# Row normalisation on one Trainium2 core: tiles of 16 rows in three buffers, with sums and scaling shared by two engines

## The chip, the core and the metric

The kernel runs on one NeuronCore of one Trainium2 chip. The metric is the device time of the slowest (here the only) core in microseconds (us), as the median of several executions. VectorE is called DVE in the profile, ScalarE is ACT, and the sequencers that issue transfers are SPq (loads) and ACTq (stores). The page counts 16 DMA engines for the core; on the load and the store queue they moved 67.11 MB each between HBM and the on-chip memory SBUF.

## The reference

```python
x = np.random.randn(32, 512, 1024).astype(np.float32)
sums = np.sum(np.abs(x), axis=-1, keepdims=True)
return (x / (sums + 1e-8)).astype(np.float32)
```

There are 16384 rows of 1024 numbers, so 67.11 MB are read and 67.11 MB are written. Each of the 128 partitions gets 128 rows. Below, "one row" of a tile is one row in each partition: 128 x 4 KiB = 0.524 MB.

## The kernel before

A tile takes 12 rows per partition (the last tile 8), in a ring of 4 buffers. DVE sums the absolute values of all rows and scales two thirds of them. ACT scales the rest and issues the stores.

```python
R = 12
BUFS = 4
...
def piece(flat, i):                      # a tile is one contiguous stretch of HBM:
    a, k = P * sum(rows[:i]), rows[i]    # partition p has k consecutive rows of it
    return flat[a : a + P * k, :].rearrange("(p r) d -> p r d", p=P)
...
# normalize(x_tile, 0, k, k - k // 3):
nc.vector.tensor_reduce(out=s[:, :k], in_=x_tile[:, r0 : r0 + k, :], ..., apply_absolute_value=True)
nc.vector.tensor_scalar_add(out=s[:, :k], in0=s[:, :k], scalar1=EPS)
nc.vector.reciprocal(out=inv[:, :k], in_=s[:, :k])
nc.vector.tensor_mul(...)                # rows r0 .. r0 + kv on DVE
for r in range(kv, k):
    nc.scalar.activation(out=row, in_=row, func=Copy, scale=inv[:, r : r + 1])
...
for i, k in enumerate(rows):
    x_tile = sbuf.tile([P, R, d], FP32)
    nc.sync.dma_start(out=x_tile[:, :k, :], in_=piece(x_flat, i))
    normalize(x_tile, 0, k, k - k // 3)
    nc.scalar.dma_start(out=piece(out_flat, i), in_=x_tile[:, :k, :])
```

Of the kernel before, what the change touches and what calls it, by code (L numbers as in the profile page):

```python
# [1 line left out]

# [4 lines left out]

FP32 = mybir.dt.float32
EPS = 1e-8


@with_exitstack
def kernel(
    ctx: ExitStack,
    tc: tile.TileContext,
    x: bass.AP,
    out: bass.AP,
):
    nc = tc.nc
    P = nc.NUM_PARTITIONS  # L20

    x_flat = x.flatten_outer_dims()
    out_flat = out.flatten_outer_dims()
    n, d = x_flat.shape


    R = 12
    BUFS = 4
    per_partition = n // P
    assert n % P == 0  # L30
    rows = [R] * (per_partition // R)
    if per_partition % R:
        rows.append(per_partition % R)

    def piece(flat, i):
        a, k = P * sum(rows[:i]), rows[i]
        return flat[a : a + P * k, :].rearrange("(p r) d -> p r d", p=P)

    sbuf = ctx.enter_context(tc.tile_pool(name="sbuf", bufs=BUFS))
    stats = ctx.enter_context(tc.tile_pool(name="stats", bufs=4))  # L40

    def normalize(x_tile, r0, k, kv):

        s = stats.tile([P, R], FP32)
        nc.vector.tensor_reduce(  # L45
            out=s[:, :k],
            in_=x_tile[:, r0 : r0 + k, :],
            axis=mybir.AxisListType.X,
            op=mybir.AluOpType.add,
            apply_absolute_value=True,  # L50
        )
        nc.vector.tensor_scalar_add(out=s[:, :k], in0=s[:, :k], scalar1=EPS)  # L52
        inv = stats.tile([P, R], FP32)
        nc.vector.reciprocal(out=inv[:, :k], in_=s[:, :k])  # L54
        nc.vector.tensor_mul(  # L55
            out=x_tile[:, r0 : r0 + kv, :],
            in0=x_tile[:, r0 : r0 + kv, :],
            in1=inv[:, :kv].unsqueeze(2).to_broadcast([P, kv, d]),
        )
        for r in range(kv, k):  # L60
            row = x_tile[:, r0 + r, :]
            nc.scalar.activation(  # L62
                out=row,
                in_=row,
                func=mybir.ActivationFunctionType.Copy,
                scale=inv[:, r : r + 1],
            )

    with tc.manual_schedule():
        for i, k in enumerate(rows):  # L70
            x_tile = sbuf.tile([P, R, d], FP32)
            nc.sync.dma_start(out=x_tile[:, :k, :], in_=piece(x_flat, i))  # L72
            normalize(x_tile, 0, k, k - k // 3)
            nc.scalar.dma_start(out=piece(out_flat, i), in_=x_tile[:, :k, :])  # L74


# [1 line left out]
_INS = ['x']  # L78
_OUTS = [((32, 512, 1024), 'float32')]


# [23 lines left out]
```

## Time and profile before

| | before |
|---|---|
| time, median of 3 (range) | 317.11 us (317.05 to 318.38) |
| span of the profiled run | 315.7 us |
| DVE, ACT busy | 235.8 us, 46.1 us |
| bytes, mean rate | 134.23 MB, 425 GB/s |

The span is what the profiler saw of one execution. An engine's busy time is the sum of its instructions. Here every compute engine has a busy share below 100% (DVE 75%, ACT 15%), and the DMA share is 0.97 to 1.01 from 2 to 312 us, so the kernel waits for bytes. The prediction shows the lines.

### The profile page before, as it was taken

How to read it: one execution, taken by the hardware profiler on the slowest of the kernel's cores; microseconds unless marked ns; L12 is line 12 of the kernel's file. 1: busy time of each engine (PE TensorE's matmuls, PEld its weight loads, DVE VectorE, ACT ScalarE, POOL GpSimd, SP SyncE). 2: the span in 40 equal slices, each digit the busy share in tenths (PEclk: the TensorE clock that was granted, in tenths of full speed). 3: DMA queues.
4: the chain of work that ended last, by engine and by line, in shares of the span. 5: the costliest groups of instructions: out<-in, count | busy, mean ns of one | idle time of the engine just before them, and what ended most of it. 6: DMA issues, size and time to landing. Idle time of an engine off the chain costs nothing.

```text
span 315.7 us, 205 instructions
## 1 busy us (share of the span) xinstructions
DVE 235.8 (75%) x44; ACT 46.1 (15%) x43; POOL 0.2 (0%) x4
## 2 busy tenths in 40 slices
DVE  0069999999999699739947991997399469979400
ACT  0010501303105003200500050032005000502000
POOL 0000000000000000000000000000000000000000
DMA  8999999999999999999999999999999999999996
GB/s 318 467 405 436 455 380 423 405 473 423 399 479 417 405 479 411 423 461 411 455 436 405 473 417 405 473 423 399 486 406 411 479 413 421 438 455 411 455 401 274
DMA packets 3169, 134.23 MB, mean 425 GB/s; under 512 B 352, under 2 KB 352, under 8 KB 352
## 3 DMA queue, kind: packets, MB, share of 16 engines
q1 hardware_dynamic: 1584, 67.11, 49.7%
q10 hardware_dynamic: 1584, 67.11, 49.1%
q14 instruction: 1, 0.01, 0.0%
HBM read 67.11 MB, written 67.11 MB: 425 GB/s over the span
## 4 chain that ended last, share of the span: by engine, by line
another core or an unknown queue 36%; DMA 31%; DVE 26%; SPq 0%; issue 0%; DVEq 0%; ACTq 0%
DMA x_tile<-in_x_dram 15%; DMA out_dram<-x_tile 15%; DVE s L45 15%; DVE x_tile L55 10%; SPq L72 0%; DVE inv L54 0%; DVE s L52 0%; DVEq L54 0%; ACTq L74 0%
## 5 line engine op out<-in xcount | busy, mean ns | idle before, releaser
L45 DVE TENSOR_REDUCE s<-x_tile 128x12 f32<-128x12288 f32 (+1 forms) x11 | 138.2, 12562 | 58.0 <-DMA x_tile<-in_x_dram 58.0
L55 DVE TENSOR_TENSOR x_tile<-x_tile,inv 128x8192 f32<-128x8192 f32 (+1 forms) x11 | 93.5, 8498 | 0.4
L62 ACT ACTIVATE x_tile<-x_tile,inv 128x1024 f32<-128x1024 f32 x42 | 44.9, 1137 | 226.3 <-DVE inv L54 226.3
L62 ACT ACT_TABLE_LOAD x1 | 1.3, 1283 | 18.7 <-DMA x_tile<-in_x_dram 18.7
L54 DVE RECIPROCAL inv<-s 128x12 f32<-128x12 f32 (+1 forms) x11 | 2.5, 225 | 0.9
L52 DVE TENSOR_SCALAR s<-s 128x12 f32<-128x12 f32 (+1 forms) x11 | 1.9, 173 | 0.4
L89 POOL MEMSET const-bfloat16-1.0<- 128x1 bf16 x1 | 0.1, 101 | 0.0
L89 POOL MEMSET const-uint8-127<- 128x1 uint8 x1 | 0.1, 101 | 0.0
L89 POOL MEMSET const-float32-0.0<- 128x1 f32 x1 | 0.1, 98 | 0.2 <-issue 0.2
L89 POOL MEMSET const-float32-1.0<- 128x1 f32 x1 | 0.1, 98 | 0.0
## 6 DMA issues: line engine op xcount, KB each, us to landing
x_tile<-in_x_dram SPq DMA_DIRECT2D x10, 6144.0 KB, 34.9
out_dram<-x_tile ACTq DMA_DIRECT2D x10, 6144.0 KB, 51.3
x_tile<-in_x_dram SPq DMA_DIRECT2D x1, 4096.0 KB, 30.4
out_dram<-x_tile ACTq DMA_DIRECT2D x1, 4096.0 KB, 19.1
```

The costliest lines, as they stand in the source:

```text
L45: nc.vector.tensor_reduce(out=s[:, :k], in_=x_tile[:, r0 : r0 + k, :], axis=mybir.AxisListType.X, op=mybir.AluOpType.add, apply_absolute_v ...
L52: nc.vector.tensor_scalar_add(out=s[:, :k], in0=s[:, :k], scalar1=EPS)
L54: nc.vector.reciprocal(out=inv[:, :k], in_=s[:, :k])
L55: nc.vector.tensor_mul(out=x_tile[:, r0 : r0 + kv, :], in0=x_tile[:, r0 : r0 + kv, :], in1=inv[:, :kv].unsqueeze(2).to_broadcast([P, kv, d]),)
L62: nc.scalar.activation(out=row, in_=row, func=mybir.ActivationFunctionType.Copy, scale=inv[:, r : r + 1],)
L89: nc = _bacc.Bacc("TRN2", target_bir_lowering=False, num_devices=1)
```

## The change

The intent is to take work off DVE. The absolute sums are shared: DVE sums three fifths of the rows and ACT the rest, with an Abs activation per row that accumulates its output. Scaling is halved between the two. Tiles grow to 16 rows in three buffers (the same 48 rows in flight), with a first and a last tile of 8 rows, so that stores start early and the last compute is short.

```diff
-    R = 12
-    BUFS = 4
+    R = 16
+    BUFS = 3
-    rows = [R] * (per_partition // R)
-    if per_partition % R:
-        rows.append(per_partition % R)
+    rows = [R // 2] + [R] * (per_partition // R - 1) + [R // 2]
...
+        kv = k * 3 // 5
+        km = k // 2
         nc.vector.tensor_reduce(
-            out=s[:, :k],
-            in_=x_tile[:, r0 : r0 + k, :],
+            out=s[:, :kv],
+            in_=x_tile[:, :kv, :],
...
+        for r in range(kv, k):
+            nc.scalar.activation(
+                out=junk[:, :],                 # in PSUM, never read
+                in_=x_tile[:, r, :],
+                func=mybir.ActivationFunctionType.Abs,
+                accum_out=s[:, r : r + 1],
+            )
...
         nc.vector.tensor_mul(
-            out=x_tile[:, r0 : r0 + kv, :],
+            out=x_tile[:, :km, :],
...
-        for r in range(kv, k):
+        for r in range(km, k):
```

More of the change, by code (lines that the diff above doesn't have):

```diff
@@ L24 @@
     n, d = x_flat.shape
-    R = 12
-    BUFS = 4
+    R = 16
+    BUFS = 3
     per_partition = n // P
-    assert n % P == 0
-    rows = [R] * (per_partition // R)
-    if per_partition % R:
-        rows.append(per_partition % R)
+    assert n % P == 0 and per_partition % R == 0
+    rows = [R // 2] + [R] * (per_partition // R - 1) + [R // 2]
     def piece(flat, i):
@@ L40, with normalize @@
     stats = ctx.enter_context(tc.tile_pool(name="stats", bufs=4))
-    def normalize(x_tile, r0, k, kv):
+    psum = ctx.enter_context(
+        tc.tile_pool(name="psum", bufs=1, space=bass.MemoryType.PSUM)
+    )
+    junk = psum.tile([P, d], FP32)
+    def normalize(x_tile, k):
+        kv = k * 3 // 5
+        km = k // 2
         s = stats.tile([P, R], FP32)
         nc.vector.tensor_reduce(
-            out=s[:, :k],
-            in_=x_tile[:, r0 : r0 + k, :],
+            out=s[:, :kv],
+            in_=x_tile[:, :kv, :],
             axis=mybir.AxisListType.X,
@@ L51, in normalize @@
         )
+        for r in range(kv, k):
[4 more added lines that the diff above has]
+                accum_out=s[:, r : r + 1],
+            )
         nc.vector.tensor_scalar_add(out=s[:, :k], in0=s[:, :k], scalar1=EPS)
@@ L55, in normalize @@
         nc.vector.tensor_mul(
-            out=x_tile[:, r0 : r0 + kv, :],
-            in0=x_tile[:, r0 : r0 + kv, :],
-            in1=inv[:, :kv].unsqueeze(2).to_broadcast([P, kv, d]),
-        )
-        for r in range(kv, k):
-            row = x_tile[:, r0 + r, :]
+            out=x_tile[:, :km, :],
+            in0=x_tile[:, :km, :],
+            in1=inv[:, :km].unsqueeze(2).to_broadcast([P, km, d]),
+        )
+        for r in range(km, k):
+            row = x_tile[:, r, :]
             nc.scalar.activation(
@@ L72 @@
             nc.sync.dma_start(out=x_tile[:, :k, :], in_=piece(x_flat, i))
-            normalize(x_tile, 0, k, k - k // 3)
+            normalize(x_tile, k)
             nc.scalar.dma_start(out=piece(out_flat, i), in_=x_tile[:, :k, :])
```

## The prediction

> **What bounds the kernel now.** I began with the busy shares and the DMA line of the page, and asked which of the two could fill 315.7 us.
>
> ```profile
> DVE 235.8 (75%) x44; ACT 46.1 (15%) x43; POOL 0.2 (0%) x4
> DMA packets 3169, 134.23 MB, mean 425 GB/s; under 512 B 352, under 2 KB 352, under 8 KB 352
> ```
>
> No compute engine is full. The kernel moves 134.23 MB, 67.11 in and 67.11 out, at a mean of 425 GB/s. Whether that mean has holes in it is told by the windows view, where the last two columns are the busy share of the 16 DMA engines and their GB/s (the first are the stretch, its length, then busy us of DVE, ACT, POOL):
>
> ```profile
> 0.00:2.00 2.00, 0.00 (x0) 0.00 (x0) 0.20 (x4) 1.00 1.05 295
> 2.00:40.00 38.00, 21.27 (x4) 5.55 (x5) 0.00 (x0) 1.00 0.97 418
> 40.00:60.00 20.00, 19.90 (x5) 4.27 (x4) 0.00 (x0) 1.00 1.01 413
> 60.00:120.00 60.00, 56.66 (x10) 8.53 (x8) 0.00 (x0) 1.00 1.01 437
> 120.00:180.00 60.00, 46.09 (x9) 8.53 (x8) 0.00 (x0) 1.00 1.00 434
> 180.00:240.00 60.00, 45.69 (x12) 8.70 (x9) 0.00 (x0) 1.00 1.00 433
> 240.00:280.00 40.00, 30.92 (x6) 8.37 (x8) 0.00 (x0) 1.00 1.00 433
> 280.00:312.00 32.00, 15.27 (x4) 2.19 (x2) 0.00 (x0) 1.00 0.99 429
> 312.00:316.00 4.00, 0.00 (x0) 0.00 (x0) 0.00 (x0) 1.00 0.15 66
> ```
>
> From 60 us to 280 us the transfers never stop: share 1.00, about 434 GB/s. All bytes at 434 GB/s are 134.23 / 0.434 = 309.3 us, so only 315.7 - 309.3 = 6.4 us of the span are not bytes at the steady rate. They sit at the two ends: the start and the loads-only stretch (2 to 60 us, slightly under rate), and the last 4 us at 66 GB/s. The second check is the tile period, read from the timeline of DVE:
>
> ```profile
> 139.07 12.95 DVE L45 TENSOR_REDUCE s<-x_tile 128x12 f32<-128x12288 f32 x1 [6.76 <-DMA x_tile<-in_x_dram]
> 168.08 12.95 DVE L45 TENSOR_REDUCE s<-x_tile 128x12 f32<-128x12288 f32 x1 [6.80 <-DMA x_tile<-in_x_dram]
> 197.08 12.95 DVE L45 TENSOR_REDUCE s<-x_tile 128x12 f32<-128x12288 f32 x1 [6.78 <-DMA x_tile<-in_x_dram]
> ```
>
> Starts are 29.0 us apart. A tile of 12 rows (one row here is 128 x 4 KB = 0.524 MB) in and out is 24 x 0.524 = 12.58 MB, which at 434 GB/s is 29.0 us: the period is the bytes alone. DVE works 22.1 us of it and waits 6.8 us for a load. The tail could still be a compute path, so I read the timeline there:
>
> ```profile
> 277.61 0.34 ACTq L74 DMA_DIRECT2D out_dram<-x_tile  x1
> 279.65 8.69 DVE L45 TENSOR_REDUCE s<-x_tile 128x8 f32<-128x8192 f32 x1 [2.13 <-DMA x_tile<-in_x_dram]
> ...
> 288.88 6.56 DVE L55 TENSOR_TENSOR x_tile<-x_tile,inv 128x6144 f32<-128x6144 f32 x1
> 295.53 0.34 ACTq L74 DMA_DIRECT2D out_dram<-x_tile  x1
> ```
>
> The last load lands at 279.6, and the last store is issued at 295.5, after 15.9 us of reduce, small steps and scaling. But the store issued at 277.6 (12 rows, 14.5 us alone) stands behind a remainder of the one before, and the windows show share 0.99 from 280 to 312. So the last tile's compute hides behind stores, though the chain of waits passes through it.
>
> [...] when a load and a store are both queued I give each half the rate. The trace agrees roughly: loads of 6.29 MB land in a median of 34.9 us, about twice the 14.5 us of one alone plus latency. [...] The pitch goes from 48 KiB (12 rows) to 64 KiB here; the trace before cannot show the new pitch. [...] the trace has 1137. I take as much for the new Abs activations, with some 0.1 us on top for the accumulator, an allowance of mine.
>
> **The change part by part.** The durations come from the groups by form:
>
> ```profile
> L45 DVE TENSOR_REDUCE s<-x_tile 128x12 f32<-128x12288 f32 x10 | 129.5, 12950 | 55.9 <-DMA x_tile<-in_x_dram 55.9
> L55 DVE TENSOR_TENSOR x_tile<-x_tile,inv 128x8192 f32<-128x8192 f32 x10 | 86.9, 8692 | 0.3
> L62 ACT ACTIVATE x_tile<-x_tile,inv 128x1024 f32<-128x1024 f32 x42 | 44.9, 1137 | 226.3 <-DVE inv L54 226.3
> L45 DVE TENSOR_REDUCE s<-x_tile 128x8 f32<-128x8192 f32 x1 | 8.7, 8685 | 2.1 <-DMA x_tile<-in_x_dram 2.1
> ```
>
> *Sums.* A reduce costs (12950 - 8685) / 4 = 1066 ns a row plus 158 ns. Of 16 rows DVE takes 9: 9.75 us. ACT takes 7 at about 1.2 us: 8.4 us, beside it. *Scaling.* DVE takes 8 rows, 8.69 us as in the row above; ACT 8 rows at 1.07 us back to back, 8.5 us, beside it. Between the phases lie 0.5 us (31.58 to 32.08 in the timeline of before). A 16-row tile thus takes 9.75 + 0.5 + 8.7 = 19.0 us, where 12 rows took 22.1. An 8-row tile takes 4 rows each: about 4.8 + 0.5 + 4.4 = 9.7 us; the first one 1.3 us more for the table load.
> *Busy time.* DVE: 7 x (9.75 + 8.69) + 2 x (4.42 + 4.42) + 9 x 0.4 = 150 us instead of 236. ACT: 57 sums at 1.2 plus 64 scalings at 1.07 plus 1.3 = 138 us instead of 46. All of it lies beside transfers.
> *Transfers.* The bytes don't change. There are 18 issues instead of 22. Period of a tile: 32 x 0.524 / 0.434 = 38.7 us, of which 19.0 are compute.
> *Buffers.* 3 x 16 rows hold as many rows as 4 x 12. Load i+3 waits for store i. I followed the queues by hand at 1.208 us a row, half rate each when both have work, 1.9 us from last byte to start of work (16.7 computed for the first load of before, 18.6 seen). First load landed 13.8; first store issued about 25 instead of 40.9; third load still running when the first store has landed (47), so no hole at the start. In the steady state, from the end t of store i-1: load i+2 is issued at t+2, load i+1 finishes its remaining 3 rows at t+7.3 and is seen at t+9.2, its compute ends at t+28.2, and store i, already queued, ends at t+38.7. So the next store is queued 10 us early, and the DMA engines always have a store or a load. At the end: last load seen at about 277, last store issued at about 287, the 16-row store ahead of it ends at about 301. Again queued, by 14 us.
> *Sum.* First bytes at about 2.2 us + 256 + 256 rows: 134.23 MB / 0.434 = 309.3 us, to 311.5; the final receipt and end as before (312.5 to 315.7), 3 us; start imbalance of 0.5 to 1.5 us. Span 315.2, times about 1.4 us more outside the span (317.11 - 315.7): 316.6 us. The 86 us of DVE time that go buy next to nothing.
>
> **Rivals.** (1) *The earlier first store and the shorter last compute are gains.* They are 15 us and 6 us sooner; were both on the path, 317 - 21 = 296 us. Against it: 309.3 us of bytes at a share of 1.00. What can be won is only part of the 6.4 us at the ends. (2) *Three buffers starve the queues.* Then each of six or seven tiles would show a hole; 2 us each makes 330 us. For it: a load now waits for a store of 16 rows, and one buffer fewer is in flight. Against: 10 us of margin. Even if the ACT sums ran after the DVE sums (they share the tile s), compute would be 27.4 us and the margin still about 2 us; rows of x_tile are already scaled by both engines at once in the trace, so parts of a tile are tracked. (3) *The 64 KiB rows move at another rate.* Each per cent is 3 us; nothing in the trace speaks for it. (4) *ACT becomes a bound and delays its own store issues*, as they stand in its stream behind 16 activations: 16.9 us of ACT work in 38.7 us, no.
>
> **Range and chances.** A DMA-bound kernel whose bytes stay is fixed to within its ends: 309.3 + 4.4 at best is 313.7 of time, and the repeats of before reach 318.4. I take 315.0 to 318.8. Faster by over 2% means below 310.8, some 1.5 us over the bytes alone: 1%. Slower by over 2% (323.5) needs rival 2 or 3: 3%.
>
> **What would show it.** Right: share about 1.00 and 433 to 437 GB/s from 60 to 280 us; reduces 38.7 us apart; DVE near 150 and ACT near 138 us busy; DVE waits for loads some 20 us a tile; last store issued over 5 us before the one ahead of it lands. Wrong: stretches with a share below 0.95 between 60 and 280 us, placed after a store's landing (rival 2), or a share of 1.00 at fewer GB/s (rival 3); sums one after the other on DVE and ACT would show a smaller margin only.

## The result, and the profile after

| | before | after |
|---|---|---|
| time, median of 4 (range) | 317.18 us (317.05 to 318.38) | 321.60 us (319.84 to 321.73) |
| span of the profiled run | 315.7 us | 319.9 us |
| DVE, ACT busy | 235.8, 46.1 us | 150.6, 134.3 us |
| mean rate over the span | 425 GB/s | 420 GB/s |

The ratio is 1.0118 with a 95% interval of 1.0075 to 1.0161. Ratios here are the mean time of one kernel's fast runs over that of the other's of the same rounds, so not quite the ratio of the quoted medians. The change is "same" at the 2% mark, but it is 4.4 us slower, where 0.6 us faster was predicted, and it lies outside the predicted range.

The first lines of the page of the changed kernel, busy shares and DMA packets:

```profile
DVE 150.6 (47%) x36; ACT 134.3 (42%) x179; POOL 0.2 (0%) x4
DMA packets 2594, 134.24 MB, mean 420 GB/s; under 512 B 288, under 2 KB 288, under 8 KB 288
```

The compute side came out as intended. The groups of instructions by form (line, engine, operation, shapes, count, then busy us and mean ns, then idle time before them) say so in detail:

```profile
L50 DVE TENSOR_REDUCE s<-x_tile 128x9 f32<-128x9216 f32 x7 | 68.3, 9755 | 124.7 <-DMA x_tile<-in_x_dram 124.7
L74 ACT ACTIVATE x_tile<-x_tile,inv 128x1024 f32<-128x1024 f32 x64 | 67.5, 1135 | 15.9 <-DVE inv L66 15.9
L58 ACT ACTIVATE junk<-x_tile 128x1024 f32<-128x1024 f32 x57 | 58.6, 1027 | 151.1 <-DMA x_tile<-in_x_dram 149.6
L58 ACT ACTIVATION_READ_ACCUMULATOR junk<-x_tile 128x1 f32 x57 | 10.6, 186 | 0.0
```

The reader sees 9.755 us for nine rows (9.75 predicted), and 57 sums on ACT that cost two instructions each. Both engines wait over 120 us in all for loads, so neither is a bound.

The windows view of the changed kernel has the DMA share and GB/s in its last two columns:

```profile
60.00:120.00 60.00, 35.18 (x8) 30.63 (x42) 0.00 (x0) 1.00 1.01 436
120.00:180.00 60.00, 21.44 (x5) 18.77 (x25) 0.00 (x0) 1.00 1.01 435
180.00:240.00 60.00, 36.67 (x8) 32.12 (x44) 0.00 (x0) 1.00 0.97 422
240.00:280.00 40.00, 19.31 (x5) 16.90 (x23) 0.00 (x0) 1.00 1.01 433
280.00:312.00 32.00, 9.86 (x5) 9.24 (x13) 0.00 (x0) 1.00 1.00 430
312.00:320.00 8.00, 0.00 (x0) 0.00 (x0) 0.00 (x0) 1.00 0.12 53
```

By this view the engines are busy as before. (A window's edge cuts packets of 1 MB over the 16 engines, so 0.97 and 422 in one window prove no hole.) What is new is the last line: after 312 us little moves, for seven more microseconds. In the kernel before, the span ended at 315.7.

The timeline of DVE shows the tile period and the end:

```profile
103.52 9.75 DVE L50 TENSOR_REDUCE s<-x_tile 128x9 f32<-128x9216 f32 x1 [20.06 <-DMA x_tile<-in_x_dram]
...
261.59 9.75 DVE L50 TENSOR_REDUCE s<-x_tile 128x9 f32<-128x9216 f32 x1 [20.52 <-DMA x_tile<-in_x_dram]
```

```profile
280.73 0.34 ACTq L86 DMA_DIRECT2D out_dram<-x_tile  x1
292.49 1.03 ACT L58 ACTIVATE junk<-x_tile 128x1024 f32<-128x1024 f32 x1 [12.12 <-DMA x_tile<-in_x_dram]
292.49 4.42 DVE L50 TENSOR_REDUCE s<-x_tile 128x4 f32<-128x4096 f32 x1 [11.85 <-DMA x_tile<-in_x_dram]
...
302.17 0.34 ACTq L86 DMA_DIRECT2D out_dram<-x_tile  x1
```

Four periods take 158.1 us, 39.5 us each where 38.7 was predicted, and the last load is seen at 292.5 where about 277 was predicted. Yet no view shows an idle DMA engine.

**Where the 4 us are.** The compute starts on a tile when all 16 DMA engines have done their share of its load (the last load's 16th increment of the semaphore came at 292.47 us, and DVE started at 292.49), and the trace keeps the moment of each engine's increment. None of the views prints them; I read them from the records of the trace. Stores of the changed kernel, with the median engine and the delay of the last one, in us:

```
store of tile        1      2      3      4      5      6      7      8 (last)
median engine     97.96 136.61 175.26 213.90 250.11 281.53 303.28 313.19
last - median      0.70   1.95   2.75   3.23   6.61   7.23   6.09   5.85
```

In the kernel before, the last store lands at 313.56 in the median and 1.11 us later on its last engine (stores in mid-run: 0.4 to 0.5 us; loads 2.4 to 2.8 us, which does not grow). So the median engine of the changed kernel is even 0.4 us earlier than before, with a period of 38.65 us as predicted, and the whole loss is in a few engines that fall behind: 319.04 against 314.67 us for the last landing, 4.4 us.

An engine falls behind by slow packets. Each packet here is one partition's contiguous run (the seven 16-row tiles of 128 partitions, in and out, are 1792 packets of 64 KiB in the trace). In the changed kernel a packet of 64 KiB takes 2.418 us in the median, 27.1 GB/s. After 62 us, 69 packets took longer, by up to 0.93 us, with 14.6 us of excess in sum over the 16 engines. In the kernel before (packets of 48 KiB, 1.815 us) there are 12 such packets with 1.0 us. In what follows this sum is called the **slow time**: the excess of all packets that start after 62 us over the median of their length, where it is over 15 ns. (Before 62 us the excess is 29.6 us in the kernel before and 23.8 in the changed one, so the loss does not come from there.) Sorted into chains by their ends and starts (packets of one engine follow each other within 10 ns), the packets show 16 engines with 72 load and 72 store packets each, with work from the first byte to the last, nearly without a gap, and the latest one with 7.0 us of excess, 1.4 of it before 62 us.

### The profile page after: what moved, and what is told of

Read it like the earlier page. It is cut to its first block, busy times and chain, and to the rows that moved or that the text cites. A ratio compares the mean times of both kernels' runs of the same rounds, so it can differ in the third digit from the quotient of the medians.

```text
span 319.9 us, 321 instructions
## 1 busy us (share of the span) xinstructions
DVE 150.6 (47%) x36; ACT 134.3 (42%) x179; POOL 0.2 (0%) x4
## 2 busy tenths in 40 slices
DMA packets 2594, 134.24 MB, mean 420 GB/s; under 512 B 288, under 2 KB 288, under 8 KB 288
## 4 chain that ended last, share of the span: by engine, by line
another core or an unknown queue 49%; DMA 36%; DVE 7%; ACT 1%; SPq 1%; issue 1%; DVEq 0%; ACTq 0%
DMA x_tile<-in_x_dram 22%; DMA out_dram<-x_tile 13%; DVE x_tile L67 4%; DVE s L50 3%; ACT junk L58 1%; SPq L84 1%; DVE inv L66 0%; DVE s L64 0%; DVEq L64 0%; ACTq L86 0%
## 5 line engine op out<-in xcount | busy, mean ns | idle before, releaser
L50 DVE TENSOR_REDUCE s<-x_tile 128x9 f32<-128x9216 f32 (+1 forms) x9 | 77.1, 8569 | 149.6 <-DMA x_tile<-in_x_dram 149.6
L58 ACT ACTIVATE junk<-x_tile 128x1024 f32<-128x1024 f32 x57 | 58.6, 1027 | 151.1 <-DMA x_tile<-in_x_dram 149.6
L74 ACT ACTIVATE x_tile<-x_tile,inv 128x1024 f32<-128x1024 f32 x64 | 67.5, 1135 | 15.9 <-DVE inv L66 15.9
L67 DVE TENSOR_TENSOR x_tile<-x_tile,inv 128x8192 f32<-128x8192 f32 (+1 forms) x9 | 69.7, 7743 | 0.3
L58 ACT ACTIVATION_READ_ACCUMULATOR junk<-x_tile 128x1 f32 x57 | 10.6, 186 | 0.0
L66 DVE RECIPROCAL inv<-s 128x16 f32<-128x16 f32 (+1 forms) x9 | 2.2, 242 | 0.3
L64 DVE TENSOR_SCALAR s<-s 128x16 f32<-128x16 f32 (+1 forms) x9 | 1.6, 174 | 1.4 <-ACT junk L58 0.6
```

Of the source, the lines that this page charges most:

```text
L50: nc.vector.tensor_reduce(out=s[:, :kv], in_=x_tile[:, :kv, :], axis=mybir.AxisListType.X, op=mybir.AluOpType.add, apply_absolute_value=True,)
L58: nc.scalar.activation(out=junk[:, :], in_=x_tile[:, r, :], func=mybir.ActivationFunctionType.Abs, accum_out=s[:, r : r + 1],)
L67: nc.vector.tensor_mul(out=x_tile[:, :km, :], in0=x_tile[:, :km, :], in1=inv[:, :km].unsqueeze(2).to_broadcast([P, km, d]),)
L74: nc.scalar.activation(out=row, in_=row, func=mybir.ActivationFunctionType.Copy, scale=inv[:, r : r + 1],)
```

## The experiments

Eighteen kernels ran, all correct in their output, each timed beside the kernel before on its chip; the median of before stayed between 317.25 and 317.51 us. "Spread" is the delay of the last engine behind the median in the last store. "Hole" is the time from 4 us to the last store's landing on its median engine in which fewer than 8 of the 16 engines had a packet. The expectations name theories by letters: T and S, the tiles as such; C, the shared compute; P and P2, the length of the packets (64 KiB alone, or long ones in general); B and B2, three large buffers, or only lengths near 64 KiB; F, the instruction fetch; L, engines that read and write in step.

| run | tiles, buffers | packets | time, us | ratio, 95% interval | spread | slow time | hole |
|---|---|---|---|---|---|---|---|
| before | 12 rows, 4 | 48 KiB | 317.11 | | 1.11 | 1.0 | 0.0 |
| after | 16 rows, 3 | 64 KiB | 321.60 | 1.012, 1.008 to 1.016 | 5.85 | 14.6 | 0.1 |
| after_again | 16, 3 | 64 | 321.65 | 1.012, 1.010 to 1.014 | 5.21 | 12.8 | 0.4 |
| e2_old_tiles | 12, 4 | 48 | 317.63 | 1.001, 1.000 to 1.002 | 1.19 | 1.2 | 0.0 |
| g4_tiles_alone | 16, 3 | 64 | 326.91 | 1.029, 1.027 to 1.031 | 0.10 | 58.9 | 7.2 |
| e7_rows12_3 | 12, 3 | 48 | 317.71 | 0.999, 0.996 to 1.003 | 0.08 | 1.3 | 1.4 |
| e6_rows8 | 8, 6 | 32 | 317.23 | 0.999, 0.998 to 1.001 | 1.91 | 1.6 | 0.0 |
| e4_halves | 16, 3 | 32 | 318.88 | 1.005, 1.004 to 1.006 | 1.38 | 24.0 | 0.0 |
| e5_halves_pitch | 16, 3 | 32 | 318.79 | 1.004, 1.003 to 1.005 | 1.57 | 19.3 | 0.0 |
| h3_quarters | 16, 3 | 16 | 318.77 | 1.004, 1.003 to 1.006 | 0.91 | 0.9 | 0.0 |
| m1_pad | 16, 3 | 32 | 318.64 | 1.004, 1.003 to 1.005 | 1.30 | 21.0 | 0.0 |
| m2_nopad | 16, 3 | 64 | 321.09 | 1.012, 1.008 to 1.016 | 3.44 | 28.2 | 1.1 |
| h1_rows14 | 14, 3 | 56 | 319.90 | 1.008, 1.007 to 1.010 | 1.62 | 8.0 | 2.3 |
| g2_early_fetch | 16, 3 | 64 | 321.62 | 1.012, 1.010 to 1.014 | 3.62 | 14.2 | 0.0 |
| e3_rows15 | 15, 3 | 60 | 326.02 | 1.025, 1.021 to 1.029 | 0.10 | 5.0 | 7.3 |
| h2_rows15_tail | 15, 3 | 60 | 334.54 | 1.042, 1.036 to 1.047 | 0.10 | 27.4 | 11.2 |
| h4_rows12_first8 | 12, 3 | 48 | 326.55 | 1.030, 1.028 to 1.031 | 0.09 | 26.6 | 8.6 |
| e9_first12 | 16, 3 | 64 | 325.83 | 1.025, 1.020 to 1.029 | 0.07 | 37.9 | 3.9 |
| k8 | 16, 3 | 64 | 335.03 | 1.055, 1.051 to 1.060 | 3.50 | 142.3 | 0.3 |
| k16 | 16, 3 | 64 | 337.69 | 1.063, 1.058 to 1.067 | 2.07 | 143.6 | 0.0 |

Times are medians of all runs; ratios are of fast runs alone. A run over 1.5% above the fastest of its kernel counts as slow. Three rows hold such runs: e3_rows15 has one (fast median 325.09 us), g2_early_fetch one (321.59), and h2_rows15_tail four of six (its two fast runs took 328.61 and 332.55); of the runs of before beside h1 to h4 one was slow, at 322.02. The slow time of k8 and k16 includes 42 and 86 us of the extra store's own packets.

(In the runs with a hole of 3.9 us or more the spread is 0.07 to 0.10 us: late engines catch up in the hole, as I read it.)

### The changed kernel again

No edit.

> The changed kernel once more, beside the experiments on the same chip. It was 1.2% slower than the kernel before (321.6 against 317.2 us). In its trace the 16 DMA engines finish their part of the last store at 313.2 us in the median and one of them 5.9 us later, where in the kernel before the spread is 1.1 us. If the late engine belongs to the kernel: 319.8 to 321.8 us again, spread of the last store's landings 4 to 7 us. If it was an accident of one chip: about 317 us and a spread near 1 us.

Measured: 321.65 us, a spread of 5.21 us. The late engine belongs to the kernel and is no accident of one run.

### The new compute on the old tiles

```diff
-    R = 16
-    BUFS = 3
+    R = 12
+    BUFS = 4
```

> The new division of sums and scaling over both engines, with the tiles of before (12 rows, 4 buffers). Theory T (the transfers of the 16-row tiles make some DMA engines slow): 317 us as before or up to 0.5 us less, last store's landings within 1.5 us. Theory C (both engines reading and writing the tile slow the transfers): 320 us or more with the late engine there.

Measured: 317.63 us, spread 1.19, slow time 1.2 us. Theory C falls: sharing sums and scaling costs the transfers nothing, and it gains nothing either. The loss comes with the tiles.

### The new tiles with the old compute

The tiles, buffers and order of the change, with DVE summing all rows and scaling two thirds.

> The other half of the change: the tiles of after (8, seven of 16, 8; three buffers) with the compute of before (vector engine sums all rows and scales two thirds). It takes about 29.6 us a tile, just about the margin of a 38.7 us period, so at most small holes. Theory F (an 8 KB instruction fetch, which the trace shows on one DMA engine at 71 us in the changed kernel and at 230 us in the kernel before, puts that engine out of step; with 16-row tiles it then keeps losing time): no fetch near 71 us as ScalarE has few instructions, so no late engine before the fetch (near 200 us or later), spread of the last store's landings under 3 us, 316.5 to 319 us. Theory S (the tiles as such): slow packets from 65 us on as in the changed kernel, 320 us or more.

Measured: 326.91 us. The expectation of theory F was wrong in the time: the only instruction fetch in mid-run came at 294.7 us, as it said, and no store landed over 2.4 us late on its last engine, but the slow time is still 58.9 us, 3.7 us per engine. Besides, there is a hole near the end, in a windows view of this run:

```profile
240.00:288.00 48.00, 38.61 (x8) 10.61 (x10) 0.00 (x0) 1.00 0.99 423
288.00:295.00 7.00, 7.00 (x2) 0.00 (x0) 0.00 (x0) 1.00 0.30 128
```

DVE is busy through the hole: the last 16-row tile takes from 263.9 to 293.6 us, and its store can't be issued before. So the 16-row tiles need the shared compute: with the old compute they cost 9.4 us, with the shared one 4.4. (The shared compute doesn't need the tiles, as the run before showed.)

### Fewer buffers alone

```diff
-    R = 16
+    R = 12
-    rows = [R // 2] + [R] * (per_partition // R - 1) + [R // 2]
+    rows = [R] * (per_partition // R) + [per_partition % R]
```

These are the tiles of before (ten of 12 rows, one of 8) in three buffers.

> The tiles of before (12 rows) and the new compute, but three buffers instead of four. Theory L: the number of buffers matters only through the phase; with mixed reads and writes 317 to 318 us, with engines in step 319 us or more and slow packets in the trace. Theory S in the form that three buffers do it: 320 us or more whatever the phase. A hole in the transfers would need the compute of a tile (14.4 us for 12 rows by the measured row times) to exceed the margin of a period of 29 us; not expected.

Measured: 317.71 us, slow time 1.3 us, a hole of 1.4 us before the last store. Three buffers alone do not make slow packets.

### The length of a row block: 60 KiB

```diff
-    R = 16
+    R = 15
-    rows = [R // 2] + [R] * (per_partition // R - 1) + [R // 2]
+    rows = [11] + [R] * 7 + [12]
```

> Three buffers of 15 rows (a first tile of 11 rows and a last of 12), the rest as in the changed kernel: runs of 60 KiB per partition instead of 64 KiB. Theory P (the 64 KiB run, a power of two, is what slows single packets): 316.5 to 318 us, landings of the last store within 1.5 us. Theory B (three large buffers, transfers of 8 MB in step, whatever their exact length): 320 to 322 us as in the changed kernel.

Measured: 326.02 us, slower than either forecast, so theory P (that exactly 64 KiB is bad) gets no support. But most of the loss is of my making:

```profile
299.00:306.00 7.00, 5.88 (x1) 5.67 (x6) 0.00 (x0) 1.00 0.31 130
```

For 7 us the transfers stand nearly still: the last load was seen at 290.1 us, 7.0 us after its median engine, and a last tile of 12 rows needs 15 us of compute, while the store ahead of it ended at about 299 in the median. I then ran it with another tail:

```diff
+    rows = [8] + [R] * 7 + [7, 8]
```

> The 15-row run again with a tail that leaves no hole: tiles of 8, seven times 15, 7 and 8 rows. The earlier one had 326.0 us, of which a hole of about 7 us in the stores before its last tile of 12 rows was part. Theory P2: 319 to 322 us with slow packets in the trace; theory B2 with 64 KiB alone: 317 to 318.5 us.

Measured: 334.54 us (328.61 and 332.55 in the two fast runs), with a larger hole, so this test of the length failed too:

```profile
304.00:315.00 11.00, 9.22 (x4) 8.86 (x12) 0.00 (x0) 1.00 0.07 31
```

The store of 7 rows was too short to cover the last load and compute. Both runs do show a late engine with 60 KiB packets (7.0 and 6.5 us late in the last load), but their times measure the tail.

### 14 rows

```diff
+    R = 14
+    rows = [8] + [R] * 8 + [8]
```

> Three buffers, tiles of 8, eight times 14, and 8 rows: packets of 56 KiB. Theory P2 (long packets lose, growing with the length): between the 12-row and 16-row times, 318 to 320.5 us. Theory B2 (only the lengths near or at 64 KiB lose): 317 to 318 us. If it is as slow as 16 rows (321 or more), the length between 48 and 56 KiB would be the threshold.

Measured: 319.90 us, between 12 and 16 rows as theory P2 has it. Slow time is 8.0 us; one engine was 7.0 us late in the last load, and a hole of 2.3 us in the stores followed from that.

### A first tile of 8 rows with 12-row tiles

```diff
+    R = 12
+    rows = [8] + [R] * 9 + [4, 8]
```

> Three buffers of 12 rows with a first tile of 8 (tiles 8, nine times 12, 4, 8): packets of 48 KiB, but the short first tile and the pause between the first and second store of the changed kernel. Theory P2: 317 to 318.5 us, no late engine. If the first tile sets off the slow packets: 320 us or more.

Measured: 326.55 us. Until 260 us the slow time is 3.0 us in sum, and no engine falls behind as in the changed kernel, so the early store and the pause after it are not the cause. The time is lost at the end: slow packets of 24 us in sum after 260 us, where 12-, 4- and 8-row transfers meet, and a hole of 8.6 us with the same cause as in the 15-row run (a store of 4 rows covers nothing). As a test of the total time it failed.

### Halves, with and without the pitch

Each load and each store of a 16-row tile becomes two of 8 rows; in the first version each half is contiguous in HBM, in the second a half takes 8 of the 16 rows of every partition.

```diff
-            nc.sync.dma_start(out=x_tile[:, :k, :], in_=piece(x_flat, i))
+            for h, part in halves(x_flat, i):
+                nc.sync.dma_start(out=x_tile[:, h : h + H, :], in_=part)
```

> The 16-row tiles and three buffers stay, but each load and store is two transfers of 8 rows, each with its own contiguous stretch of memory: runs of 32 KiB. Theory P (64 KiB exactly): back to 316.5 to 318 us. If any power of two does it: 319 us or more. Theory B (three buffers of 16 rows): 320 to 322 us, since the buffers and the waits are unchanged.

> As the run with halves, but the layout of the 16-row tile in HBM stays: each transfer takes 8 of the 16 rows of each partition, so packets of 32 KiB at a pitch of 64 KiB. If the packet length (32 KiB) decides: like the halves, about 318.9 us. If the pitch in HBM decides: 320 us or more, like the changed kernel.

Measured: 318.88 and 318.79 us. The pitch in HBM (32 or 64 KiB per partition) makes no difference here: 0.09 us between the medians. The late engine is gone (spreads of 1.4 and 1.6 us). A slow time of 19 to 24 us remains, but it is shared: nearly all of it falls in one episode between 105 and 120 us, in which all engines lose about 1.3 us, and none is late afterwards.

### Quarters

As the halves, with H = R // 4.

> The 16-row tiles and three buffers, each load and store as four transfers of 4 rows: packets of 16 KiB. Halves (32 KiB packets) had 318.9 us. Theory P2: 317 to 318.5 us. If the 16-row tile with its three buffers itself costs the rest, as with the halves: 318.7 us or more.

Measured: 318.77 us with a slow time of 0.9 us. Slow packets are gone, so theory P2 held there; its forecast of the time missed, because packets of 16 KiB cost more per byte in this trace. One takes 0.611 us, and 512 of them per engine at that time less the 4 ns by which neighbours overlap are 310.8 us. For 256 packets of 32 KiB at 1.213 us it is 309.5 us.

### Smaller tiles

```diff
+    R = 8
+    BUFS = 6
+    rows = [R] * (per_partition // R)
```

> The new compute with 16 tiles of 8 rows and 6 buffers: as many rows in flight, packets of 32 KiB. Theory F with the loss growing with the packet length: 317 to 318.5 us and a spread of landings under 2.5 us. If every division into blocks of a power of two rows loses: 319 us or more, as with the halves (318.9).

Measured: 317.23 us, slow time 1.6 us. 8-row tiles match the kernel before.

### Do the engines run in step?

In the changed kernel the 16 engines alternate between load and store together: from 100 to 140 us there are at most one or at least 14 engines in a load packet for 85% of the time. In the kernel before this is 13%. I took this for the cause (theory L) and tried to break it with an extra store.

```diff
+            if i == 1:
+                nc.scalar.dma_start(out=spare[:, :, :], in_=x_tile[:K, :, :])   # K = 8 or 16
```

The spare tensor lies in HBM and is never read.

> The changed kernel with one extra store of 16 rows of 8 partitions to a spare tensor in HBM, issued just before the store of the second tile. It goes to 8 of the 16 DMA engines, one packet of 64 KiB each (2.42 us of their time), and leaves those 8 writing while the other 8 read. Theory L (packets turn slow where all engines alternate between load and store in step; where half read and half write they don't): hardly any slow packets after 65 us (under 2 us in sum over the engines, against 13 and 14 us in the two traces of the changed kernel), and the 8 engines end 2.4 us after the others, at about 315.3 us, so about 318.3 us. Theory S (the slow packets come of the 16-row tiles or the three buffers as such): as many slow packets, 321.6 us or more, up to 324.

> The control: the same extra store, but 16 partitions, so one extra packet on each of the 16 engines; they stay in step. Theories L and S both: slow packets stay (8 us or more after 65 us), a late engine stays, and the time is that of the changed kernel plus 2.4 us, about 324 us. If instead this one too comes to about 319 us, the extra store acts in another way than by the phase, and theory L falls.

Measured: 335.03 and 337.69 us. Both expectations were wrong, and the experiment doesn't decide anything, because the extra store was no simple kick: its packets took 7.4 to 8.1 us (8 partitions) and 7.2 to 8.9 us (16) instead of 2.42. That is 3.0 to 3.7 times as long. I had not expected it, and it is not shown why: stores from so few partitions occur in these two runs alone. The extra store moved what was meant: the pages count 0.52 and 1.04 MB more than that of the changed kernel (134.76 and 135.28 MB), and 8 and 16 more packets under 512 B (296 and 304 against 288, which is 16 for each of its 18 transfers), as for 8 and 16 engines. After this jolt slow packets went on for some 70 us in both, and in the first they came back at 190 us.

As the whole cause, theory L falls by other runs. With 8-row tiles the engines are in step for 65% of the time from 100 to 140 us, with three buffers of 12 rows for 45%, and both have almost no slow packets. And this run has mixed reads and writes from 60 us on, with 37.9 us of slow time:

```diff
+    rows = [12] + [R] * 7 + [4]
```

> The changed kernel with a first tile of 12 rows and a last of 4 instead of 8 and 8. Theory L with the phase set early by the spread of the engines' first packets: if the 48 KiB first packets spread the engines as widely as in the kernel before, reads and writes mix and the time is 316.5 to 318.5 us. If the engines stay in step: 320 to 322 us. Theory S: 320 to 322 us. The share of time in which nearly all engines read, or nearly all write, in the trace tells which.

Measured: 325.83 us. The engines did leave the common step, and it was worse, not better: 34.5 us of the slow time fall between 62 and 100 us. After that, however, slow packets nearly stop. From 100 to 250 us they sum to 0.5 us here (engines in step for 9% of that time), against 5.4 and 6.4 us in the two traces of the changed kernel (63% and 60%). The first 15-row run has 0.5 us too (8%), but the second has 3.1 (12%), and the tiles with the old compute 15.9 (29%). So it is not excluded that long packets keep turning slow while the engines run in step; no run sets the step alone. Some 3.9 us of it are a hole before the last store, as the tail is again small (4 rows).

### The instruction fetch

In both traces of the changed kernel an 8 KiB transfer of the instruction queue comes at 71.0 us and takes 0.309 us on one DMA engine. In the first trace, by the chains of packets, it is that engine which then falls behind. In the second it is not: there the latest engine is one without a fetch, 2.6 us behind at 158 us, when the engine with the fetch was 0.4 behind. In the kernel before the fetch comes at 230.1 us.

```diff
+        for _ in range(55):
+            nc.scalar.activation(out=junk[:, :1], in_=dot[:, :], func=mybir.ActivationFunctionType.Abs)
```

> The changed kernel with 55 one-element activations on ScalarE at the start, where it waits for the first load. They move the first instruction fetch from 71 us into the loads-only stretch before 15 us, and the second from 287 to about 195 us. Theory F: hardly any slow packets between 30 us and 190 us (under 0.5 us in sum; 7 us in the changed kernel), the late engine begins at about 195 us, and the time drops by 1 to 3 us to 318.5 to 320.5. Theory S: slow packets from 65 us on, time unchanged at 321.6.

Measured: 321.62 us with a wide range, 319.96 to 325.60 (the last in the slow state, the fast ones up to 321.73); the profiled run was the fastest of them. The fetches moved to 16.9 and 197.1 us. Slow time between 62 and 180 us was 4.0 us, between those of the two traces of the changed kernel (4.6 and 3.2; the 7 us of the expectation were a wrong sum), though spread over many engines, and an episode of 8.2 us followed at 220 to 230 us. Taking the early fetch away did not give the time back, and the run with the tiles alone had slow packets without any fetch. As the cause of the loss theory F falls.

### The length of the packets alone

The last pair has equal tiles, buffers, transfers, waits and instructions. They differ in one number: a gap of 128 bytes in SBUF after each 8 rows of a tile, which cuts each run of 64 KiB in two.

```diff
-            x_tile = sbuf.tile([P, R, d], FP32)
+            x_tile = sbuf.tile([P, 2, H * d + PAD], FP32)      # PAD = 32 numbers, or 0
```

(To keep instructions from crossing the gap, ACT sums 8 rows of 16 instead of 7 in both.)

> The changed kernel with a gap of 128 bytes after the first 8 rows of each tile in SBUF, one transfer per tile as before (ScalarE sums 8 of 16 rows instead of 7, so that no instruction crosses the gap). The trace should show packets of 32 KiB. Theory P2 (packet length): no engine late by over 2.5 us at the end, 317 to 319 us. If the number of transfers mattered and not the packet length: 320.5 us or more, as the changed kernel.

> The control: the same with no gap, so packets of 64 KiB. Both theories: a late engine by 3 us or more in the last store's landings and 320 to 322.5 us as in the changed kernel. If it comes to 318 us, the one row moved from VectorE to ScalarE was the cause and the packet length isn't shown.

The packet lines of the two pages, with the gap first:

```profile
DMA packets 4386, 134.24 MB, mean 424 GB/s; under 512 B 288, under 2 KB 288, under 8 KB 288
```

```profile
DMA packets 2594, 134.24 MB, mean 420 GB/s; under 512 B 288, under 2 KB 288, under 8 KB 288
```

The gap turned 1792 packets of 64 KiB into 3584 of 32 KiB (4386 - 2594 = 1792 more) and changed the time from 321.09 to 318.64 us, with intervals of the ratio that do not touch (1.0075 to 1.0158, and 1.0025 to 1.0051). The spread fell from 3.44 to 1.30 us. The gap also moves the second half of a tile and the later buffers by 128 bytes and more in SBUF. That this is not what helps is shown by the two runs with halves, which cut the packets without a gap and came to 318.88 and 318.79 us. So the length of the packets is shown to cost time here: 2.45 us by the medians, and 0.8 to 4.2 us by the ends of the two intervals, as the runs without the gap scatter from 318.79 to 323.34 us. What changed in the traces is less the sum of the slow time (28.2 us without the gap, 21.0 with it) than how evenly the engines share it. They also fell out of step: from 100 to 250 us they are in step for 46% of the time without the gap and 7% with it. So the pair does not tell whether a long packet is hit as such, or because long packets keep the engines in step. What is left with the gap, 318.64 against 317.30 us, answers to its slow time: 21.0 us over 16 engines are 1.3 us each, nearly all in episodes at 100 to 110 and 130 to 135 us.

## Why the prediction was wrong

By its own steps:

- **Bound and bytes.** Right. The changed kernel is bound by transfers; its median engine ends its last store at 313.2 us, 0.4 us before that of the kernel before.
- **Sums, scaling, busy time.** Right. A 16-row tile takes 19.1 us from the first reduce to the store's issue (103.52 to 122.65 us in the timeline; 19.0 predicted), DVE is busy 150.6 us (150) and ACT 134.3 (138). The sum on ACT costs 1.18 us (12.97 to 14.15 us in the timeline), not by the estimate's way, which was the 1.137 us of a scaling and some 0.1 us: the Abs activation takes 1.027 us, 0.11 less than a scaling (1.135), and the accumulator is a second instruction of 0.186 us.
- **Period.** Right for the median engine (38.65 us between landings of stores), wrong for the kernel, which waits for the last engine and has 39.5 us between starts.
- **Rivals.** Rival 1 was rightly refused: no part of the 21 us came. Rival 4 (ACT as a bound) too. Rival 2 named "three buffers starve the queues". In the changed kernel they don't, and with 12 rows three buffers cost nothing (0.999). Rival 3, "the 64 KiB rows move at another rate", was dismissed with "nothing in the trace speaks for it". This is the one that happened, in a form that the prediction had not thought of: the usual packet keeps its rate, and single packets on single engines lose up to 0.9 us.
- **The step that failed** is the sum: "134.23 MB / 0.434 = 309.3 us, to 311.5; the final receipt and end as before". It treats 16 engines as one pipe. In the trace each engine has its own 144 of the packets, so the end is that of the slowest one, 5.9 us behind the median; twelve engines were done by 313 us and took over none of its work. The mean share of 1.00 could not show it. The sum has a term for an imbalance at the start ("0.5 to 1.5 us") and none for a spread at the end. The size of what is missing is the difference of the two last landings, 4.4 us.
- **The margin at the end.** Predicted 14 us; measured about 1 us (the last store was issued at 302.17, and the store ahead of it landed at 303.28 in the median). The lag enters twice: the last load was issued at 256.8 instead of 250.7 us, as the store that frees its buffer landed 6.6 us late on one engine, and it was itself 8.5 us late on its last engine.
- **Slips.** The rows are 128 in and 128 out, not "256 + 256"; the bytes were right. The first store landed at 54.7, not 47 us; no hole followed.

What is shown: the loss comes with the tiles and not with the compute, in the changed kernel it sits in late DMA engines, and cutting the packets from 64 to 32 KiB takes away about two thirds of it by the medians (2.45 of 3.8 us in that pair), and two other ways of cutting them came to nearly the same time. Packets of 48 KiB in ten 12-row tiles had next to no slow time in three runs; 56 KiB lay between in time. The slow time does not grow evenly with the length (8.0 us at 56 KiB, 5.0 and 27.4 at 60). What is open: why a long packet is hit at all, and whether the common step has a part in it. Slow packets come in episodes: before 62 us (23.8 us of excess in the changed kernel), at 105 to 120 us with the halves, at 220 to 230 us with the early fetch, for some 70 us after the extra store. No run shows why they start or stop. The records don't name the engines, so it is not known which ones fall behind. Open as well is the shared loss of 1.3 us that 16-row tiles keep with 32 KiB packets and 8-row tiles don't have.

No version beat the kernel before. 8-row tiles in six buffers (0.999) and the old tiles with the new compute (1.001) equal it, which fits the DMA share of 0.97 to 1.01 from 2 to 312 us that it already had.

## What to carry to other kernels

When transfers bound a kernel, ask not only for the mean DMA share but for the last engine: compare the landings of a transfer's 16 parts, and see whether the spread grows from tile to tile. Larger tiles bought nothing here and cost time: runs of 32 and 48 KiB per partition (tiles of 8 rows, and of 12 with a last one of 8) took 317.11 to 317.71 us, runs of 56 and 64 KiB in tiles of 14 and 16 rows with the shared compute 319.90 and 321.60 us, and a gap of 128 bytes in SBUF was enough to cut the longest (318.64 us with it, 321.09 without). With few buffers, see that a large store stands ahead of a last tile whose compute is short: last tiles of 12 rows, of 7 and 8, of 4 and 8, and of 4 opened holes of 4 to 11 us here.
